# Two transformer blocks on one core: who issues four DRAM copies, who rounds four one-hot tiles, and where the big tiles lie

## The chip, the cores and the metric

One core of one Trainium2 chip runs the whole program. The time is the device time of one execution, in microseconds (us); lower is better. Before the change three executions gave 2247.26 us as their median (2241.52 to 2248.51).

## The reference, cut to what matters

The input is 512 rows of 1024 numbers, all float32. The first block scales and shifts the normalised rows by factors that come from six large "ada" products, projects them with `w_in`, and feeds three mixers: a recurrent one (rwkv), a causal attention with decay (fox) and a sparse attention (nsa). It then projects out and runs a convolutional feed-forward layer. The second block is feed-forward, a token mixer of three more attentions, and feed-forward again.

Four of the attentions add a bias that depends only on the distance between query and key, looked up in a small table of 32 buckets:

```
dist = qpos[:, None] - kpos[None, :]
bias = rel_bias[t5_bucket(dist)]
logits = einsum(q, k) * scale + bias
```

So a bias tile of 128 queries by n keys holds in each row the same line, moved by one element from row to row.

The feed-forward layers are the bulk of the work:

```
u = h @ w_up;  gate, val = split(u);  out = (silu(gate) * val) @ w_down
```

## The kernel before, in words

**Matrix products.** To keep float32 accuracy each operand is split into a high and a low part of a rounded type (float32r), and each product is three matmuls: high by high, low by high, high by low. A weight chunk of 128 x 1024 comes by one DMA into a tile `raw` (three buffers), ScalarE rounds it into `whi` (L273), VectorE or GpSimd makes the rest `wlo` (L274). `Weights.next` does this, and every chunk waits on SyncE's queue for the buffer it will fill. A helper `mm` (L284) issues all matmuls. In `dense` the moving operand of the matmul is an activation: `uh`/`ul` (inputs of a layer), `hh`/`hl` (hidden values of a feed-forward layer, moved in its down product), `oh`/`ol` (attention outputs, in the branch products), `yh`/`yl` (in the output product of the second mixer).

**Ada.** `some_ada` (called between the steps of rwkv) loads 512 KB pieces of the ada weights through the same `raw` buffers, multiplies them on VectorE (`am`, L299), ScalarE and GpSimd (L507, L508, L512), and sums over partitions by a matmul of 128 x 1.

**Bias lines.** `lines` makes the lines: for each 512 columns it loads a one-hot matrix of 33 rows into a tile `lo` (L467), rounds it to float32r (`CAST`, L469), multiplies it by the bias table on TensorE (`pss` in the first block, `lps` in the second), evacuates on ScalarE and stores to a DRAM tensor `d` (L475). There are four such steps in the first block (called from `decays`, beside rwkv) and six in the second (called from `bias_2`, in the first feed-forward layer's up product). `skew` (L477) then copies each line 128 times within DRAM, so that later a DMA can read it back with a step of one element less than a row and get the moved rows. There are four such copies: `k1` (6 lines of 639 numbers, 768 rows written), `k2` (8 lines of 639, 1024 rows), `ka0` (4 lines of 1785, 512 rows of 7140 bytes) and two small ones `ka1` and `ka2` (4 lines of 255 each, 512 rows each). The attentions read them much later: `tb<-k` (L1174) and `bt<-k` (L1614).

**What sets the order.** The engines run their instruction streams in order, and each waits at its next instruction until its inputs are there. A scheduler of the tile framework fixes the order in each stream, so a small change in the code moves neighbours too. All DMAs but four small ones are issued by SyncE, in one stream (`SPq` in the rows), weights and copies alike; GpSimd issues none.

**Where tiles lie.** Pools take room in SBUF one after the other; the `st` pool stands ahead of most others. In the built program of before the tiles `raw`, `whi`, `wlo`, `uh` and `ul` start at multiples of 256 bytes within a partition, `hh` and `hl` 192 bytes past one, `oh`, `ol`, `yh` and `yl` 224 bytes past one.

Of the kernel before, what the change touches and what calls it, by code (L numbers as in the profile page):

```python
# [10 lines left out]
F32 = mybir.dt.float32  # L11
# [7 lines left out]
P = 128  # L19
# [260 lines left out]
def two_blocks(ctx, tc, ins, out):  # L280
    nc = tc.nc
    S, V, G, PE = nc.scalar, nc.vector, nc.gpsimd, nc.tensor
    def mm(o, l, r, start=True, stop=True):
        PE.matmul(o, l, r, start=start, stop=stop)  # L284

    def act(o, i, f, **kw):
        S.activation(o, i, f, **kw)  # L287

    def tt(o, a, b, op):
        V.tensor_tensor(o, a, b, op=op)  # L290
# [7 lines left out]
    def stt(o, a, s, b, op0, op1):  # L298
        V.scalar_tensor_tensor(o, a, s, b, op0=op0, op1=op1)  # L299
# [24 lines left out]
    def vc(name, i=0, n=1):  # L324
        s = VECS[name].start
        return vec[:, s + i:s + i + n]
# [9 lines left out]
    st = ctx.enter_context(tc.tile_pool(name="st", bufs=1))  # L336

    def tmp(name="tmp"):
        return st.tile([P, T], F32, name=name, tag="tmp", bufs=3)
# [7 lines left out]
    def row_sums(ps, accs, start=True, stop=True, s=ALL):  # L347

        n = len(blocks(s))
        for j, acc in enumerate(accs):  # L350
            for i, b in enumerate(blocks(s)):
                mm(ps[:, n * j + i:n * j + i + 1], acc[:, b * P:(b + 1) * P],
                   ones[:, 0:1], start and i == 0, stop and i == n - 1)
        return ps[:, :n * len(accs)]

    def rsq(m, name="rr"):

        n = m.shape[-1]
        v = st.tile([P, NB], F32, name="rv", bufs=2)
        ts(v[:, :n], m, EPS, None, ADD)  # L360
        r = st.tile([P, NB], F32, name=name, bufs=2)
        G.tensor_tensor(r[:, :n], v[:, :n], mhalf[:, :n], op=ALU.pow)
        return r[:, :n]
# [15 lines left out]
    def rms_bcast(psp, tag, r, name="R"):  # L379
        R = st.tile([P, T], F32, name=name)  # L380
        spread(psp, tag, r, R)
        return R
# [22 lines left out]
    def two(k):  # L405
        return slot(UTAG[2 * k], "uh", F32R), slot(UTAG[2 * k + 1], "ul", F32R)
# [8 lines left out]
    def cut_by(t, g, b, hl, s=ALL):  # L415

        h, l = hl[0][:, s], hl[1][:, s]
        if b is None:
            act(h, t, AF.Copy, scale=g)
            stt(l, t, g, h.bitcast(F32), MUL, SUB)  # L420
        else:
            act(h, t, AF.Identity, bias=b)
            stt(l, t, b, h.bitcast(F32), ADD, SUB)
        return hl
# [9 lines left out]
    def dense(ps, hi, lo, k0, us, start=True, stop=True, w=P, s=ALL):  # L434

        n, ps = len(us), ps[:, s]
        for k, (uh, ul) in enumerate(us):
            uh, ul = uh[:, s], ul[:, s]
            a, b = hi[:, k0 + k * w:k0 + k * w + w], lo[:, k0 + k * w:k0 + k * w + w]
            mm(ps, a, uh, start and k == 0, False)  # L440
            mm(ps, a, ul, False, False)
            mm(ps, b, uh, False, stop and k == n - 1)
# [13 lines left out]
    def lines(name, pool, o_tile, pst, rb, n, h, dst):  # L456

        l = pool.tile([33, h], F32, name="rb" + name)
        V.memset(l[32:33, :], 1.0)
        nc.sync.dma_start(l[:32, :], ins[rb])  # L460
        hi, lo = [pool.tile([33, h], F32R, name="rb" + name + c) for c in "hl"]
        act(hi, l, AF.Copy)
        tt(lo, l, hi.bitcast(F32), SUB)
        for j in range(0, n, 512):
            m = min(512, n - j)
            o = o_tile(F32)[:33, :m]
            nc.sync.dma_start(o, ins["lines" + name][:, j:j + m])  # L467
            E = o_tile(F32R)[:33, :m]
            G.tensor_copy(E, o)  # L469
            ps = pst()[:h, :m]  # L470
            mm(ps, hi, E, True, False)
            mm(ps, lo, E, False, True)
            o = o_tile(F32)[:h, :m]
            act(o, ps, AF.Copy)
            nc.sync.dma_start(dst[:, j:j + m], o)  # L475

    def skew(name, src, row0, rows, rstep, off, n):  # L477

        d = dram.tile([rows, P, n], F32, name=name)
        s = src[:]  # L480
        w = s.shape[1]
        nc.sync.dma_start(d, bass.AP(tensor=s.tensor, offset=s.offset + row0 * w + off, ap=[[rstep * w, rows], [0, P], [1, n]]))
        return d

    def skewed(d, h, nh, off, ap):
# [5 lines left out]
    def ada(dst, sec, k, raw, ap, bufs, late):  # L491

        am = [ap.tile([P, 256], F32, name=f"am{q}", bufs=bufs) for q in range(2)]
        n = 4 if late else AN
        for q in range(2):
            aw = raw()
            nc.sync.dma_start(aw.rearrange("p a b -> p (a b)"), ins["ada"][sec, k][:, q * 1024:(q + 1) * 1024])
            for r in range(4):
                s = sil[:, 4 * q + r:4 * q + r + 1]
                if q == 0 and r:  # L500
                    stt(am[0], aw[:, r], s, am[0], MUL, ADD)
                elif q == 0:
                    ts(am[0], aw[:, 0], s, None, MUL)
                elif r == 0:
                    act(am[1], aw[:, 0], AF.Copy, scale=s)
                elif late:
                    G.tensor_scalar(aw[:, r], aw[:, r], s, 1.0, op0=MUL, op1=MUL)  # L507
                    G.tensor_tensor(am[1], am[1], aw[:, r], op=ADD)  # L508
                elif r < n:
                    act(aw[:, r], aw[:, r], AF.Copy, scale=s)  # L510
                    G.tensor_tensor(am[1], am[1], aw[:, r], op=ADD)
        G.tensor_tensor(am[1], am[0], am[1], op=ADD)  # L512
        for s in range(2):
            c = slice(s * P, (s + 1) * P)
            for r in range(n, 4):
                mm(dst[s], aw[:, r, c], sil[:, 4 + r:5 + r], r == n, False)
            mm(dst[s], am[1][:, c], ones[:, 0:1], n == 4, True)
# [20 lines left out]
    with tc.tile_pool(name="lin", bufs=1) as lin, tc.tile_pool(name="p0", bufs=1, space=PSUM) as p0:  # L538
        x0 = part
        for i in range(4):  # L540
            nc.sync.dma_start(x0[:, 2 * i:2 * i + 2], ins["x"][:, 2 * i:2 * i + 2])
        q0 = SqSum()
        for k in range(8):
            q0.add(x0[:, k])
        ps = row_sums(p0.tile([P, T], F32, name="nst", tag="x0"), [q0.acc])
        msx = const.tile([P, NB], F32, name="msx")
        V.tensor_copy(msx, ps[:, :NB])
        R = rms_bcast(p0, "x0", rsq(msx))
        kps = [p0.tile([P, T], F32, name=f"k{m}") for m in range(7)]
        gm = st.tile([P, 8], F32, name="gf")  # L550

        def modulate(k):

            ps = p0.tile([P, T], F32, name="mps", tag="x0")
            ada([ps[:, 0:1], ps[:, 1:2]], 0, k, lambda: lin.tile([P, 4, 256], F32, name="aw", bufs=AWB), lin, 3, False)
            tt(mod[:, k:16:8], ps[:, :2], vc("ada_b", 0, 16)[:, k::8], ADD)
            stt(gm[:, k:k + 1], mod[:, 8 + k:9 + k], 1.0, vc("norm_g", k), ADD, MUL)

        for k in range(8 + LA):
            if k < 8:  # L560
                modulate(k)
            if k < LA:
                continue
            k -= LA
            t = tmp("uf")
            stt(t, x0[:, k], gm[:, k:k + 1], R, MUL, MUL)
            us.append(cut_by(t, None, mod[:, k:k + 1], two(k)))
            hi, lo = W.next("rwkv")
            for m in range(7):
                dense(kps[m], hi, lo, m * P, us[k:k + 1], k == 0, k == 7)  # L570
        for m in range(7):
            act(pr[m], kps[m], AF.Identity, scale=omu[:, m:m + 1])
            stt(pr[m][:, 1:], kps[m][:, :T - 1], vc("mu", m), pr[m][:, 1:], MUL, ADD)
# [4 lines left out]
    def bank(tag, n):  # L578
        return psm.tile([P, T], F32, name="ps" + tag, tag="p" + tag, bufs=n)
# [669 lines left out]
    gf = st.tile([P, 8], F32, name="gf")  # L1249
# [48 lines left out]
    pst, psd, psa, n = bank("t", 2), bank("t", 2), bank("o", 2), 0  # L1298
# [186 lines left out]
    op = blk.enter_context(tc.tile_pool(name="op", bufs=1, reuse_waits="tile"))  # L1485
# [50 lines left out]
        for i in range(2):  # L1536
            evac(i, pn[i])

    gqk = op.tile([P, 3], F32, name="gqk")
    tt(gqk, vc("gain", 0, 6)[:, 0::2], vc("gain", 0, 6)[:, 1::2], MUL)  # L1540
    ts(gqk, gqk, -0.125, None, MUL)

# [213 lines left out]
    with tc.tile_pool(name="cc", bufs=1, reuse_waits="tile") as cc:  # L1756
# [8 lines left out]
        for i in range(1, NB):  # L1765
            n = (i + 1) * P
# [19 lines left out]
        for j in range(2):  # L1786
# [6 lines left out]
            for i in range(NB):  # L1793
                n = (i + 1) * P
# [19 lines left out]
    ap = bc.enter_context(tc.tile_pool(name="ap", bufs=1, reuse_waits="tile"))  # L1814
# [18 lines left out]
    for h in range(4):  # L1833
        po = pO()
        bias = bias_line(k2, h)
        for i in range(NB):
            n = (i + 1) * P
# [14 lines left out]
        o = tmp("ob")  # L1852
# [23 lines left out]
    for j in range(2):  # L1876
# [30 lines left out]
        o = tmp("oa")  # L1907
# [97 lines left out]
```

## Time and profile before

| what | value |
|---|---|
| median of three executions | 2247.26 us (2241.52 to 2248.51) |
| the profiled execution | 2244.32 us, of which the span of its instructions is 2242.5 us |
| TensorE (PE) matmul | 2150.2 us busy, 96% of the span |
| VectorE (DVE) | 1166.0 us, 52% |
| ScalarE (ACT) | 797.9 us, 36% |
| GpSimd (POOL) | 464.6 us, 21% |
| DMA | 238.29 MB moved, mean 106 GB/s |

"Busy" says that an engine has an instruction in work; matmuls overlap each other, so a busy TensorE may still be slower than it could be. What tells that is the distance between the starts of two matmuls. Idle time of an engine that is not the bottleneck costs nothing.

### The profile page before, as it was taken

To read this page: it belongs to the slowest core of one execution; us is meant where nothing else is said; L and a number is where in the kernel's file an instruction comes from. 1 tells how busy PE (TensorE), PEld (TensorE's weight loads), DVE (VectorE), ACT (ScalarE), POOL (GpSimd) and SP (SyncE) were. 2 spreads that over 40 slices of the span, in tenths; PEclk is the share of its full clock that TensorE was granted. 3 is DMA by queue.
4 is the path that set the end of the run, shared out by engine and by line. 5 is a ranking of instruction groups with operands and counts; after the bars stand their busy time and mean duration, and the time that the engine had idled before them with its cause. 6 is when DMAs were issued, how large, how long until landed. Compare 5 with 4: busy or idle time off the path is not lost.

```text
span 2242.5 us, 31600 instructions
## 1 busy us (share of the span) xinstructions
PE 2150.2 (96%) x12444; PEld 1761.4 (79%) x12444; DVE 1166.0 (52%) x2213; ACT 797.9 (36%) x1358; POOL 464.6 (21%) x458
## 2 busy tenths in 40 slices
PE   5988999997979999999999999999999999999999
PEld 4866776666758888878888889998877888888887
DVE  8563444667634465654334438976645455433432
ACT  5432333552523343332123335455444233222321
POOL 5044342334000000131011023242221022100110
PEclk9988998997989999999999999999999999999999
DMA  7246234200433222122222334243161223222222
GB/s 271 86 137 200 96 132 131 58 11 22 163 130 110 94 95 98 70 95 94 94 102 96 115 124 130 95 142 95 66 183 67 95 84 104 100 97 94 94 96 83
DMA packets 83321, 238.29 MB, mean 106 GB/s; under 512 B 10666, under 2 KB 19168, under 8 KB 83044
## 3 DMA queue, kind: packets, MB, share of 16 engines
q1 hardware_dynamic: 82452, 235.69, 31.3%
q8 instruction: 98, 1.61, 0.3%
q10 hardware_dynamic: 720, 0.57, 0.1%
q14 instruction: 51, 0.42, 0.1%
HBM read 216.02 MB, written 15.33 MB: 103 GB/s over the span
## 4 chain that ended last, share of the span: by engine, by line
PE 88%; DMA 6%; DVE 4%; POOL 1%; ACT 1%; issue 1%; SPq 0%; DVEq 0%; POOLq 0%; ACTq 0%
PE mm L284 65%; PE psm L284 5%; PE psr L284 4%; DMA raw<-in_wst_dram 3%; PE pS L284 3%; PE pss L284 2%; PE pO L284 2%; PE pso L284 2%; PE k L284 1%; DMA raw<-in_ada_dram 1%; PE pT L1590 1%; PE pst L1052 1%; PE psa L284 1%; DMA aw<-in_ada_dram 1%; PE pT L1573 1%
## 5 line engine op out<-in xcount | busy, mean ns | idle before, releaser
L273 ACT ACTIVATE whi<-raw 128x1024 fp32r<-128x1024 f32 (+4 forms) x314 | 327.3, 1045 | 838.3 <-PE mm L284 624.3
L274 DVE TENSOR_TENSOR wlo<-raw,whi 128x1024 fp32r<-128x1024 f32 (+4 forms) x302 | 371.5, 1232 | 358.1 <-ACT whi L273 348.3
L284 PE MATMUL mm<-uh,whi 128*128 128x512 f32 (+1 forms) x1296 | 499.5, 391 | 18.8 <-ACT whi L273 15.4
L284 PE MATMUL mm<-ul,whi 128*128 128x512 f32 (+1 forms) x1296 | 504.2, 390 | 5.3 <-DVE ul L299 5.3
L284 PE MATMUL mm<-uh,wlo 128*128 128x512 f32 (+1 forms) x1296 | 504.2, 390 | 1.6 <-DVE wlo L274 1.6
L284 PEld LDWEIGHTS mm<-uh,whi 128*128 128x128 f32 x1296 | 245.1, 191 | 72.2 <-ACT whi L273 17.4
L284 PEld LDWEIGHTS mm<-ul,whi 128*128 128x128 f32 x1296 | 246.4, 190 | 58.5 <-DVE ul L299 8.0
L284 PEld LDWEIGHTS mm<-uh,wlo 128*128 128x128 f32 x1296 | 246.2, 190 | 53.0 <-DVE wlo L274 3.6
L284 PE MATMUL mm<-hl,whi 128*128 128x512 f32 (+1 forms) x550 | 211.6, 385 | 0.0
L284 PE MATMUL mm<-hh,wlo 128*128 128x512 f32 (+1 forms) x550 | 211.6, 385 | 0.0
L284 PE MATMUL mm<-hh,whi 128*128 128x512 f32 (+1 forms) x550 | 210.7, 385 | 0.0
L1441 POOL TENSOR_TENSOR gg<-gg,R 128x512 f32<-128x512 f32 x44 | 76.8, 1748 | 477.6 <-ACT gg L287 477.6
L284 PE MATMUL mm<-whi,uh 128*128 128x256 f32 (+1 forms) x488 | 140.5, 288 | 0.0
L284 PE MATMUL mm<-whi,ul 128*128 128x256 f32 (+1 forms) x488 | 139.7, 286 | 0.0
L284 PE MATMUL mm<-wlo,uh 128*128 128x256 f32 (+1 forms) x488 | 139.2, 285 | 0.0
L284 PEld LDWEIGHTS mm<-hl,whi 128*128 128x128 f32 x550 | 102.9, 187 | 23.6
L284 PEld LDWEIGHTS mm<-hh,wlo 128*128 128x128 f32 x550 | 102.9, 187 | 23.5
L284 PEld LDWEIGHTS mm<-hh,whi 128*128 128x128 f32 x550 | 102.9, 187 | 23.3
L287 ACT ACTIVATE p<-p,smin 128x128 f32<-128x128 f32 (+4 forms) x136 | 81.8, 602 | 74.1 <-DVE smin L1028 38.6
L290 DVE TENSOR_TENSOR gh<-mm,gg 128x512 f32<-128x512 f32 x44 | 30.4, 691 | 130.8 <-PE mm L284 125.3
L284 PEld LDWEIGHTS mm<-whi,ul 128*128 128x128 f32 x488 | 93.1, 191 | 1.7 <-issue 1.5
L284 PEld LDWEIGHTS mm<-whi,uh 128*128 128x128 f32 x488 | 93.0, 191 | 1.3 <-issue 0.4
(506 smaller groups left out, 3407.0 us busy)
## 6 DMA issues: line engine op xcount, KB each, us to landing
raw<-in_wst_dram SPq DMA_DIRECT2D x294, 512.0 KB
raw<-in_ada_dram SPq DMA_DIRECT2D x32, 512.0 KB
aw<-in_ada_dram SPq DMA_DIRECT2D x16, 512.0 KB
raw<-in_wst_dram SPq DMA_DIRECT2D x8, 448.0 KB
ka<-d SPq DMA_DIRECT2D x1, 3570.0 KB
k<-d SPq DMA_DIRECT2D x1, 2556.0 KB
part<-in_x_dram SPq DMA_DIRECT2D x4, 512.0 KB
xa<-in_x_dram SPq DMA_DIRECT2D x8, 256.0 KB
```

Of the source, the lines that this page charges most:

```text
L273: nc.scalar.activation(hi[:, :n], w, AF.Copy)
L274: (e or nc.vector).tensor_tensor(lo[:, :n], w, hi[:, :n].bitcast(F32), op=ALU.subtract)
L284: PE.matmul(o, l, r, start=start, stop=stop)
L287: S.activation(o, i, f, **kw)
L290: V.tensor_tensor(o, a, b, op=op)
L1052: PE.transpose(ps[:, j:j + P], p[:, j:j + P], ident)
L1441: G.tensor_tensor(g, g, R, op=MUL)
L1573: PE.transpose(ps[:, (j * nb + b) * P:(j * nb + b + 1) * P], xn[:, (b * n + j) * P:(b * n + j + 1) * P], ident)
L1590: PE.transpose(ps[:, j:j + P], p[:, o + j:o + j + P], ident)
```

## The change

Three edits. The copies of `skew` are issued by GpSimd instead of SyncE. In `lines` the rounding of the one-hot columns is done by VectorE for the first block (name "1"); the second block stays on GpSimd. Two small tiles are allocated wider and used as before, which moves the tiles allocated behind them.

```diff
@@ -466,7 +466,7 @@
             o = o_tile(F32)[:33, :m]
             nc.sync.dma_start(o, ins["lines" + name][:, j:j + m])
             E = o_tile(F32R)[:33, :m]
-            G.tensor_copy(E, o)
+            (V if name == "1" else G).tensor_copy(E, o)
             ps = pst()[:h, :m]
@@ -479,7 +479,7 @@
         d = dram.tile([rows, P, n], F32, name=name)
         s = src[:]
         w = s.shape[1]
-        nc.sync.dma_start(d, bass.AP(tensor=s.tensor, offset=s.offset + row0 * w + off, ap=[[rstep * w, rows], [0, P], [1, n]]))
+        G.dma_start(d, bass.AP(tensor=s.tensor, offset=s.offset + row0 * w + off, ap=[[rstep * w, rows], [0, P], [1, n]]))
         return d
@@ -547,7 +547,7 @@
-        gm = st.tile([P, 8], F32, name="gf")
+        gm = st.tile([P, 24], F32, name="gf")[:, :8]
@@ -1536,7 +1536,7 @@
-    gqk = op.tile([P, 3], F32, name="gqk")
+    gqk = op.tile([P, 64], F32, name="gqk")[:, :3]
```

Places of tiles in the two built programs, as bytes past a multiple of 256:

| tiles | before | changed |
|---|---|---|
| `raw`, `whi`, `wlo`, `uh`, `ul` | 0 | 0 |
| `hh`, `hl`, `cv`, `part`, `xa`, `xb` (rows of the first and second block's layers) | 192 | 0 |
| `oh`, `ol`, `yh`, `yl`, `bt`, `av`, `xn` (second mixer) | 224 | 0 |
| rwkv's own tiles (`X`, `XT`, `Tm`, `AK`, `WU`) | 0 | 64 |
| tiles of nsa (`qs`, `tb`, `p`, `pt`) | 96 | 160 |

How the instruction streams move. First SyncE's stream in the up product of the first feed-forward layer, at the last of the second block's bias lines (`raw` are weight loads, `d` the lines, `ka` the copies):

```order
 L467 DMA lo<-in_lines_dram 33x374
 L475 DMA d_5927<-lo 20x512
-L269 DMA raw<-in_wst_dram 128x1024
-L482 DMA ka_5997<-d_5927 512x1x1785
-L269 DMA raw<-in_wst_dram 128x1024
+L269 DMA raw<-in_wst_dram 128x1024 x2
 L475 DMA d_5927<-lo 20x374
-L269 DMA raw<-in_wst_dram 128x1024
-L482 DMA ka_5999<-d_5927 512x1x255
-L482 DMA ka_6001<-d_5927 512x1x255
-L269 DMA raw<-in_wst_dram 128x1024 x109
+L269 DMA raw<-in_wst_dram 128x1024 x110
```

The copies have left the stream, and the weight loads behind them follow each other. The same place in GpSimd's stream (`tmp` is the last step ahead of the feed-forward layer, `rr` the first one at its end):

```order
 L1277 TENSOR_TENSOR tmp<-part,R_5289 128x512 x8
-L469 CAST lo<-lo 33x512 x5
+L469 CAST lo<-lo 33x512 x3
+L482 DMA k_5995<-d_5927 1024x1x639
+L469 CAST lo<-lo 33x512 x2
 L469 CAST lo<-lo 33x374
+L482 DMA ka_5997<-d_5927 512x1x1785
+L482 DMA ka_5999<-d_5927 512x1x255
+L482 DMA ka_6001<-d_5927 512x1x255
 L362 TENSOR_TENSOR rr<-rv,mhalf 128x2
```

`k2` now stands ahead of the last three roundings, the other three copies behind all of them. Third, GpSimd's stream beside rwkv (`am` are sums of an ada piece, `raw` the pieces):

```order
 L507 TENSOR_SCALAR raw<-raw,sil 128x256 x6
-L469 CAST lo<-lo 33x512
-L508 TENSOR_TENSOR am_1731<-am_1731,raw 128x256 x3
+L508 TENSOR_TENSOR am_1731<-am_1731,raw 128x256
+L482 DMA k_1237<-d_93 768x1x639
+L508 TENSOR_TENSOR am_1731<-am_1731,raw 128x256 x2
 L512 TENSOR_TENSOR am_1731<-am_1730,am_1731 128x256
-L469 CAST lo<-lo 33x512
```

The roundings are gone from it, and the copy `k1` stands in the middle of one ada sum. TensorE's stream at the last of the first block's bias lines (`psr` are rwkv's small matmuls):

```order
-L284 MATMUL psr_1676<-cm,pr_113 64x64 x16
-L284 MATMUL psr_1694<-cm,pr_114 64x64 x11
+L284 MATMUL psr_1631<-cm,pr_115 64x64 x3
 L284 MATMUL pss<-lo,rb1h 6x96
 L284 MATMUL pss<-lo,rb1l 6x96
-L284 MATMUL psr_1694<-cm,pr_114 64x64 x5
+L284 MATMUL psr_1631<-cm,pr_115 64x64 x13
```

The two matmuls that need the fourth rounded tile stand some 70 small matmuls earlier than before.

## Rows read from the trace of the kernel before

**Rows 1.** The page: span, and busy time and share of each engine.

```profile
span 2242.5 us, 31600 instructions
PE 2150.2 (96%) x12444; PEld 1761.4 (79%) x12444; DVE 1166.0 (52%) x2213; ACT 797.9 (36%) x1358; POOL 464.6 (21%) x458
```

**Rows 2.** The chain that ended last, 610 to 675 us: start, us, what.

```profile
615.51 35.76 DMA raw<-in_wst_dram
...
653.69 14.93 DMA raw<-in_wst_dram
```

**Rows 3.** Timeline of SyncE's queue, 569 to 652 us: start, us, instruction.

```profile
569.97 0.73 SPq L482 DMA_DIRECT2D k<-d  x1
...
611.35 0.69 SPq L482 DMA_DIRECT2D ka<-d  x1
...
651.47 2.11 SPq L482 DMA_DIRECT2D ka<-d  x2
```

**Rows 4.** Stretches of the feed-forward layers: busy us and count by engine.

```profile
core 0: us, PE busy (x) PEld busy (x) DVE busy (x) ACT busy (x) POOL busy (x), PEclk, DMA share, GB/s
570.00:600.00 30.00, 30.00 (x131) 23.59 (x131) 16.96 (x22) 12.12 (x18) 1.40 (x1) 1.00 0.53 179
615.70:688.70 73.00, 57.94 (x233) 46.06 (x233) 29.27 (x37) 20.57 (x28) 0.00 (x0) 0.88 0.37 127
635.00:645.00 10.00, 6.22 (x28) 4.82 (x26) 0.00 (x0) 0.00 (x0) 0.00 (x0) 0.98 0.25 104
750.30:869.90 119.60, 119.60 (x529) 99.07 (x528) 70.41 (x84) 51.09 (x65) 0.00 (x0) 1.00 0.28 97
916.20:927.40 11.20, 11.20 (x100) 11.20 (x99) 4.41 (x8) 2.53 (x4) 0.00 (x0) 1.00 0.15 48
1812.50:1829.20 16.70, 16.70 (x73) 13.47 (x72) 12.59 (x14) 4.99 (x6) 8.44 (x5) 1.00 0.22 75
1829.30:1874.50 45.20, 45.15 (x193) 35.82 (x192) 25.80 (x28) 17.06 (x23) 8.52 (x4) 1.00 0.27 95
2177.10:2238.50 61.40, 61.40 (x265) 49.15 (x263) 16.98 (x18) 10.06 (x10) 0.00 (x0) 1.00 0.23 82
```

**Rows 5.** Timeline of TensorE, single matmuls of 256 and of 512 columns.

```profile
944.51 0.28 PE L284 MATMUL mm<-uh,whi 128*128 128x256 f32 x1
...
946.91 0.28 PE L284 MATMUL mm<-uh,wlo 128*128 128x256 f32 x1
...
1995.76 0.39 PE L284 MATMUL mm<-hh,whi 128*128 128x512 f32 x1
...
1999.96 0.39 PE L284 MATMUL mm<-hh,whi 128*128 128x512 f32 x1
```

**Rows 6.** Timelines beside rwkv, 169 to 190 us: SyncE's queue, GpSimd, TensorE.

```profile
169.41 0.85 SPq L482 DMA_DIRECT2D k<-d  x1
177.30 1.24 SPq L497 DMA_DIRECT2D raw<-in_ada_dram  x2
...
188.06 0.93 POOL L507 TENSOR_SCALAR raw<-raw,sil 128x256 f32<-128x256 f32 x2 [9.85 <-DMA raw<-in_ada_dram]
188.93 0.26 POOL L469 CAST lo<-lo 33x96 fp32r<-33x96 f32 x1
...
189.24 0.24 PE L284 MATMUL pss<-lo,rb1h 33*6 33x96 f32 x1 [9.46 <-POOL lo L469]
```

**Rows 7.** Stretches beside rwkv, columns as in rows 4.

```profile
180.00:190.00 10.00, 0.76 (x11) 0.60 (x12) 0.71 (x2) 0.24 (x1) 1.59 (x4) 0.69 0.57 211
190.00:198.00 8.00, 8.00 (x73) 6.46 (x70) 2.82 (x6) 3.24 (x5) 6.32 (x8) 0.54 0.52 136
```

**Rows 8.** GpSimd's timeline at 594 us, VectorE's at 118 us.

```profile
594.53 1.40 POOL L469 CAST lo<-lo 33x512 fp32r<-33x512 f32 x1 [24.76 <-DMA lo<-in_lines_dram]
...
118.04 0.43 DVE L684 COPY nr<-hr 128x512 f32<-128x512 f32 x1 [1.75 <-POOL hr L682]
```

**Rows 9.** Line L1614, the reads of `k2`: count, issue ns, first and last start.

```profile
L1614 SPq DMA_DIRECT2D bt<-k x8: 319/332/424, 1309.3 to 1549.9; - x8
```

## What the change should do to the time

> **What bounds the kernel now.** I read the page first: TensorE has a matmul in work for 96% of the span, no other engine for more than 52% [rows 1]. So time is won only where TensorE stands still, where its clock is granted at half, or where its matmuls follow each other more slowly than they could. Next I read the chain that ended last. In the feed-forward layers it is TensorE all the way, but for two pieces of 35.76 and 14.93 us that are weight loads, issued at 615.51 and 653.69 [rows 2]. SyncE's queue shows what stands just ahead of each: the copy `ka0` at 611.35 and the copies `ka1` and `ka2` from 651.47 [rows 3]. Between 635 and 645 the DMA engines are busy a quarter of the time although weights are waited for [rows 4]: the copy of 4 lines runs on 4 of 16 engines, and a weight load that needs all 16 ends only when those 4 have finished it. Third, I compared stretches in which TensorE runs without a pause, for the distance between matmuls, and the stretch beside rwkv where it stood still longest.
>
> **Term 1, the two stalls at 615 to 689.** The stretch 615.7 to 688.7 holds 232 matmuls (the count less the one that began before it) in 73.0 us. The stretch 750.3 to 869.9 has the same matmuls at 119.6/528 = 0.2265 us each [rows 4]. 232 of these take 52.5 us, so 20.5 us are lost, in standing still and at a clock of 0.88 on average. The change takes the copies off SyncE's queue and leaves TensorE's order there as it was. If a copy issued by GpSimd stands in another queue, the weights share the 4 engines with it rather than wait for its end. An estimate: the copy occupies its engines from 615.5 to about 651.3, in 512 rows, so a row takes about 35.8 x 4 / 512 = 0.28 us; a weight load puts 8 rows of 4096 bytes on an engine. Even if one row of the copy ran between any two rows of the weights, 8 rows of each would take some 3.5 us (a weight row counted at 0.16 us, from its share of the bytes), and a load is used up in 24 matmuls, 5.4 us. With three buffers that keeps up. I take the whole 20.5 us; ends 0 (still in line) and 20.5. `k2`, issued at 569.97, costs nothing now, since TensorE is busy throughout 570 to 600 [rows 3, 4].
>
> **Term 2, the place of the tiles.** In down products the moving operand `hh` lies 192 bytes past a multiple of 256, in up products `uh` lies on one. The up stretch gives 0.2265 us a matmul; the down stretch 2177.1 to 2238.5 gives 61.4/264 = 0.2326 from the window, and single starts give (1999.96 - 1995.76)/18 = 0.2333 [rows 4, 5]. Weights, stationary tiles and widths are alike. That the place is what matters and not the kind of product is shown by `oh` in the branch stretch, 16.7/72 = 0.2319, and `yh` in the output stretch, 45.2/192 = 0.2354 [rows 4]: both lie 224 bytes past a multiple, and the output product is written like an up product. The difference is 6.7 ns (0.2333 less 0.2266, as the tighter reading). Of 512 columns there are 6 down products of 8 x 11 x 3 less 66, that is 1518, with `hh`/`hl`, and 192 each with `oh` and `yh`: 1902 x 6.7 ns = 12.7 us. Against this, the 132 matmuls of 256 columns in the last two tiles of the first layer now run at 11.2/99 = 0.1131 us, while those of `uh`, on a multiple, run at (946.91 - 944.51)/20 = 0.1200: a loss of 0.9 us. Sum 11.8 us gained, as TensorE has no other pause in these stretches. The weights must then come every 5.4 us instead of 5.6, which the up stretches already do at a DMA share of 0.28 [rows 4]. Ends: 0, if the place is a coincidence, and 13. ScalarE's and VectorE's work on the moved tiles I cost at nothing, hidden behind TensorE; that of rwkv, whose tiles go from 0 to 64 bytes, stays in the bounds of term 3, as no row tells how it behaves.
>
> **Term 3, the stretch beside rwkv.** `k1` is issued at 169.41; an ada load issued behind it at 177.30 lets GpSimd go on only at 188.06, and GpSimd's fourth rounding, in line behind that ada work, comes at 188.93; TensorE's `pss` waited 9.46 us for it [rows 6]. From 180 to 190 TensorE is busy 0.76 us, and the next 8 us run at a clock of 0.54 [rows 7], so about 9.2 + 8.0 x 0.46 = 12.9 us are lost. The change removes both links: `k1` no longer stands ahead of the ada load, and the rounding, now VectorE's, no longer stands behind ada work. The four roundings cost VectorE about 4 x 0.43 = 1.7 us, by its copy of 128 x 512 [rows 8], beside rwkv's own steps. But ada work itself is still due: behind `k1` in GpSimd's stream stand the rest of an ada sum, whose small matmul TensorE takes in order, and all later sums. What is late next is that sum, and GpSimd now waits for the lines to land and issues 768 rows itself. SyncE's issue took 0.85 us; at most, if GpSimd is held until the copy is done, 18.7 us (169.41 to 188.06) [rows 6]. No row shows a copy issued by GpSimd; I take 5 us, nearer to an issue than to a transfer, with part of it on the path. Of 12.9 us I count 7 as gained. Ends: 13 gained, and 18.7 - 12.9 = 5.8 lost.
>
> In the feed-forward layer the roundings stay on GpSimd behind `k2`: the fourth begins at 594.53, 24.6 us after `k2` is issued now [rows 3, 8], so it is covered up to that hold. Behind `ka0` to `ka2` GpSimd has nothing until that layer ends, and `k2` is first read at 1309.3 [rows 9], hundreds of us later: longer copies cost nothing there.
>
> **Sum.** The profiled execution took 2244.3 us, 1.8 of them outside its span. 2244.3 - 20.5 - 11.8 - 7 = 2205.0. It lies 2.9 us below the median of the three runs and inside their range; I go one us up for that: 2206.
>
> **Rivals.**
>
> *The weights still wait (0.14).* Against the estimate of term 1: the engines are the same 16, and if each serves a long run of copy rows before it turns to the weights, the stall only changes its place. Then term 1 shrinks to between 0 and 10: 2216 to 2226. [...] The quarter share at 635 [rows 4] agrees with the common engines; no run here shows yet how two queues take turns.
>
> *The place does nothing (0.10).* Products with `hh` differ from those with `uh` also in who wrote the operand and when. Then term 2 is 0: 2217. Against it speak `oh` and `yh`.
>
> *GpSimd is held at `k1` (0.09).* As bounded above, up to the whole transfer: term 3 turns to +5.8 and the time to 2218.
>
> *Slower (0.05).* GpSimd needs so long for each row of a copy that ada sums and roundings come late. With X the time a row, `k1` holds it 768 X and `k2` 1024 X, of which 24.6 us are covered. Gains of 20.5 + 11.8 + 12.9 = 45.2 are eaten when 1792 X = 69.8 us, at X = 39 ns; the bound of 18.7 us gives 24. At 50 ns the kernel takes 2244.3 - 45.2 + 38.4 + 26.6 = 2264. [...]
>
> *No change (0.04).* The copies wait in line as before and the place does nothing: 2237 to 2250, partly within 0.3% (6.7 us), which is what a measurement of this kernel can tell from no change.
>
> **Chances and range.** The forecast, all three terms at about their size, has 0.58 and lies between 2197 (13 in terms 2 and 3) and 2212. The first three rivals are faster too: 0.58 + 0.14 + 0.10 + 0.09 = 0.91, less 0.02 for pairs of them. So faster 0.89, same 0.06, slower 0.05. The range goes from 2195 (all upper ends, at the lowest of the runs) to 2229 (the weights wait and `k1` gives nothing: 2244.3 - 11.8 - 0, less 3); about 0.15 is left out.
>
> **What would show it.** Term 1: TensorE's 232 matmuls after the last `lps` take about 53 us at full clock, and no weight load of over 10 us is left in the chain there. Term 2: matmuls with `hh`, `oh`, `yh` start 0.2265 us apart, those of 256 columns 0.120. Term 3: no wait of TensorE for a rounding, and the first NSA read of `k1` some 7 us earlier; if instead GpSimd shows a long wait or a long issue at L482, the third or fourth rival holds. The forecast is wrong if weight loads still land late while a copy runs, or if the down stretches keep 0.2333.

## The result and the profile after

| kernel | median | executions | ratio to before, 95% interval |
|---|---|---|---|
| before, timed beside it | 2244.55 us | 4 (2241.52 to 2248.51) | |
| changed | 2213.38 us | 4 (2211.90 to 2214.77) | 0.9858 [0.9844, 0.9872] |

The changed kernel is 31.2 us faster. The prediction said 2206 (2195 to 2229). The profiled execution took 2211.9 us where the sum of the prediction gave 2205.0; nearly the whole difference of 6.9 us is the third term, as the rows show.

The page of the changed kernel: span, busy time of TensorE, the DMA queues. Against [rows 1] TensorE is busy 13 us less and its share of the span has risen by one percentage point; the copies now stand in a queue of their own, `q0`.

```profile
span 2210.1 us, 31599 instructions
PE 2137.1 (97%) x12444; PEld 1764.5 (80%) x12444; DVE 1167.0 (53%) x2217; ACT 799.1 (36%) x1358; POOL 465.2 (21%) x459
...
q1 hardware_dynamic: 79098, 226.41, 30.5%
q0 software_dynamic: 5008, 9.31, 1.2%
```

**Term 1.** The chain that ended last, 600 to 680 us, in the changed kernel: start, us, what. The two pieces of weight loads of [rows 2] are gone; behind the last `lps` TensorE runs without a break.

```profile
614.95 0.45 PE lps L284 x2
615.40 64.60 PE mm L284 x284
```

**Terms 1 and 2.** Windows of the changed kernel, columns as in [rows 4], at the places that answer to its second, fifth, sixth, seventh and last row.

```profile
615.40:667.80 52.40, 52.40 (x232) 43.40 (x232) 31.70 (x39) 22.34 (x29) 2.16 (x2) 1.00 0.58 186
...
892.20:904.10 11.90, 11.90 (x100) 11.87 (x99) 4.63 (x8) 2.52 (x4) 0.00 (x0) 1.00 0.13 45
...
1785.00:1801.30 16.30, 16.30 (x74) 13.50 (x73) 12.58 (x14) 4.99 (x6) 8.30 (x4) 1.00 0.21 69
...
1801.40:1845.40 44.00, 43.89 (x193) 35.76 (x192) 26.59 (x28) 17.05 (x23) 8.42 (x4) 1.00 0.31 100
...
2146.20:2205.90 59.70, 59.70 (x265) 49.36 (x263) 16.98 (x18) 10.10 (x10) 0.00 (x0) 1.00 0.23 84
```

The matmuls after the last `lps` take 52.4 us at full clock instead of 73.0. The down stretch takes 59.7/264 = 0.2261 us a matmul by its window, which has an uncertainty of one matmul at each end. Single starts are tighter; these are from TensorE's timeline of the changed kernel, two of 256 columns and two of 512.

```profile
892.58 0.28 PE L284 MATMUL mm<-hh,whi 128*128 128x256 f32 x1
...
894.74 0.28 PE L284 MATMUL mm<-hh,whi 128*128 128x256 f32 x1
...
2160.49 0.39 PE L284 MATMUL mm<-hh,whi 128*128 128x512 f32 x1
...
2164.57 0.39 PE L284 MATMUL mm<-hh,whi 128*128 128x512 f32 x1
```

18 matmuls lie between the two of a pair: 2.16/18 = 0.1200 us at 256 columns, 4.08/18 = 0.2267 us at 512, where [rows 5] gave 0.2333. Both are the numbers that the prediction named. The windows with `oh` and `yh` have gone from 16.7 to 16.3 and from 45.2 to 44.0 us.

**Who issues the copies.** GpSimd's timeline of the changed kernel, the rows of L482, and the last line of the view of L482.

```profile
165.19 1.33 POOL L482 DMA_DIRECT2D k<-d  x1
...
569.70 1.18 POOL L482 DMA_DIRECT2D k<-d  x1 [0.42 <-DMA d<-lo]
...
610.48 1.10 POOL L482 DMA_DIRECT2D ka<-d  x1 [3.14 <-DMA d<-lo]
624.12 2.16 POOL L482 DMA_DIRECT2D ka<-d  x2 [12.54 <-DMA d<-lo]
...
DMA to landing us min/median/max: 20.6/38.7/51.5
```

An issue holds GpSimd 1.1 to 1.3 us, whether the copy has 512 or 1024 rows, and it goes on while the copy needs 20 to 50 us to land. So the third and the fourth rival fell: 1.18 us for 1024 rows is 1.2 ns a row, where 39 would have made the kernel slower.

**Term 3.** Beside rwkv the old wait is gone and another has come. SyncE's timeline of the changed kernel, 173 to 189 us, then TensorE's.

```profile
173.92 0.29 SPq L475 DMA_DIRECT2D d<-lo  x1
...
181.69 4.52 SPq L935 DMA_DIRECT2D cb<-d  x8
...
188.23 1.08 SPq L980 DMA_DIRECT2D w<-in_ck_dram  x2
```

```profile
183.61 0.91 PE L284 MATMUL psr<-X,part 64*64 64x64 f32 x22
191.65 0.66 PE L284 MATMUL psa<-kr,w 128*128 128x62 f32 x2 [7.13 <-DMA w<-in_ck_dram]
```

`cb` reads the bias lines back, so it waits until the last piece `d`, issued at 173.92, has landed (2.9 us of SyncE's waits at L935); its eight loads go out from 181.69 on, and `w`, the weights of the compression in nsa (`psa` is its matmul), stands behind them. TensorE waits 7.13 us for it at 191.65.

How much that took back is seen in one wide window, 140 to 230 us, of before and of the changed kernel, and in two pieces of the changed one.

```profile
140.00:230.00 90.00, 74.24 (x1055) 61.80 (x1054) 46.36 (x94) 24.84 (x44) 47.25 (x67) 0.89 0.57 186
```

```profile
180.00:191.70 11.70, 4.57 (x72) 3.74 (x70) 2.24 (x6) 1.89 (x4) 6.98 (x12) 0.83 0.64 183
191.70:207.00 15.30, 15.30 (x118) 13.56 (x120) 3.87 (x9) 2.82 (x3) 6.05 (x11) 0.50 0.68 227
140.00:230.00 90.00, 78.29 (x1056) 65.55 (x1056) 45.62 (x97) 24.29 (x42) 44.70 (x64) 0.85 0.58 186
```

By 230 us TensorE has begun 1055 matmuls in the one and 1056 in the other. It stood still 4 us less in the changed kernel (78.29 busy against 74.24), and gave that back in clock, 0.85 against 0.89 on average: from 191.7 to 207 it was granted 0.50 for 15.3 us behind the new wait, where [rows 7] show 8 us at 0.54 behind the old one.

Further on nothing was gained either. Of each of the next pairs the first line is from the kernel before, the second from the changed one: the reads of `k1` in nsa, then the first matmuls of the second block's bias lines, at the start of the feed-forward layer (count, ns, first and last start).

```profile
L1174 SPq DMA_DIRECT2D tb<-k x6: 326/411/589, 381.2 to 425.7; - x6
L1174 SPq DMA_DIRECT2D tb<-k x6: 327/404/587, 382.2 to 426.9; - x6
...
L284 PE MATMUL lps<-lo,rb2h x6: 340/400/402, 557.9 to 615.3; 33*20 33x512 f32 x5, 33*20 33x374 f32 x1
L284 PE MATMUL lps<-lo,rb2h x6: 347/410/410, 557.4 to 614.9; 33*20 33x512 f32 x5, 33*20 33x374 f32 x1
```

The first read of `k1` comes 1.0 us later, where the prediction expected it some 7 us earlier, and `lps` begins 0.5 us earlier.

### The profile page after: what moved, and what is told of

It reads as the page before. It is cut to its first block, busy times and chain, and to the rows that moved or that the text cites. A ratio compares the mean times of both kernels' runs of the same rounds, so it can differ in the third digit from the quotient of the medians.

```text
span 2210.1 us, 31599 instructions
## 1 busy us (share of the span) xinstructions
PE 2137.1 (97%) x12444; PEld 1764.5 (80%) x12444; DVE 1167.0 (53%) x2217; ACT 799.1 (36%) x1358; POOL 465.2 (21%) x459
## 4 chain that ended last, share of the span: by engine, by line
PE 91%; DVE 4%; DMA 3%; ACT 1%; issue 1%; POOL 1%; SPq 0%; DVEq 0%; ACTq 0%; POOLq 0%
PE mm L284 67%; PE psm L284 6%; PE psr L284 4%; PE pS L284 3%; PE pss L284 2%; PE pso L284 2%; PE pO L284 2%; PE k L284 1%; PE psa L284 1%; PE pT L1590 1%; PE pst L1052 1%; DMA aw<-in_ada_dram 1%; DMA raw<-in_wst_dram 1%; PE pT L1573 1%; DVE ul L299 1%
## 6 DMA issues: line engine op xcount, KB each, us to landing
k<-d POOLq DMA_DIRECT2D x1, 2556.0 KB, 20.6
```

## The experiments

Each was timed beside the kernel before on its chip; the medians of before there were 2246.05 (first four), 2247.53 (next four) and 2246.93 us (last four). The changed kernel's time is the one of the table above, beside 2244.55; so differences of 1 to 2 us between an experiment and the changed kernel say nothing.

**1. The second block's copies alone.**

```diff
 def skew(...):                       # kernel before
-    nc.sync.dma_start(d, ...)
+    (nc.sync if name == "k1" else G).dma_start(d, ...)
```

> The kernel before, with only the second block's four copies (k2, ka0 to ka2) issued by GpSimd; k1, the roundings and all tile places as before. TensorE's, VectorE's and ScalarE's streams are those of before. Theory (each copy stalls the weights that stand behind it in SyncE's queue): the 231 matmuls after the last lps take 52 to 53 us instead of 72.7, the time falls by 20 to 21 us to 2223.5 to 2225, and nothing else moves. Rival (the stall went only because the tiles also moved, or part of it comes back later in the layer): a gain of 10 to 17 us, 2228 to 2235.

Measured: 2227.57 us (2223.52 to 2227.64), ratio 0.9909 [0.9895, 0.9923], a gain of 18.5 us. The window behind the last `lps`:

```profile
618.80:671.00 52.20, 52.20 (x231) 43.22 (x231) 31.70 (x39) 22.36 (x29) 2.16 (x2) 1.00 0.62 188
```

The stretch is what the theory asked for, 52.2 us; the time missed its range (2223.5 to 2225) by 2.6 us. In the profiled execution what is missing lies ahead of the copies: `lps` begins at 560.9 instead of 557.9, although up to there the streams are those of before. So two executions of the same order differ by some 3 us up to that point, which the later experiments must be read against.

**2. The places alone.**

```diff
-        gm = st.tile([P, 8], F32, name="gf")
+        gm = st.tile([P, 24], F32, name="gf")[:, :8]
-    gqk = op.tile([P, 3], F32, name="gqk")
+    gqk = op.tile([P, 64], F32, name="gqk")[:, :3]
```

> The kernel before, with only the two small tiles allocated wider, so that hh, hl, oh, ol, yh, yl start at multiples of 256 bytes and rwkv's tiles 64 past one. All engine streams are those of before. Theory (the place of the moving operand sets the distance between matmuls, and rwkv's tiles don't care): 512-column matmuls with hh and oh 226.7 ns apart, the 256-column ones with hh 120, a gain of 11.5 to 12.5 us, 2232 to 2233. Rival A (the change of place costs the rwkv stretch what term 3 was to bring): the stretch up to 318 us becomes 3 to 7 us longer and the gain is only 5 to 9 us, 2235.5 to 2239.5. Rival B (the pitch in the changed kernel comes from the order and not from the place): 2244, no gain.

Measured: 2234.51 us (2231.18 to 2235.47), 0.9944 [0.9930, 0.9958], a gain of 11.5 us. The last down stretch, with the streams of before:

```profile
2167.90:2227.50 59.60, 59.60 (x265) 49.36 (x264) 16.98 (x18) 10.10 (x10) 0.00 (x0) 1.00 0.24 84
```

61.4 us have become 59.6 with no instruction moved: the place is the cause, and rivals A and B fall (`lps` begins at 556.5, so rwkv does not pay for its tiles' new place).

**3. `cb` after rwkv.** If the wait behind `cb` had eaten term 3, taking it away should give the 7 us.

```diff
 ...
         lines("1", keep, ...)
-        load_cb()
         k1.append(skew("k1", d1, 0, 6, 1, 0, LN))
 ...
     att = blk.enter_context(tc.tile_pool(name="att", ...))
+    cb = att.tile([P, 6, 55], F32, name="cb")
+    ...
+    load_cb()
```

> The changed kernel, with the eight loads of cb (L935), which in it hold SyncE's queue from 173.9 to 187 us because they wait for the last piece of d1 to land, done after rwkv into a tile of the attention's pool; tile places of all large tiles as in the changed kernel. Theory (term 3 was eaten by this wait: TensorE's psa at 191.65 waits 7.1 us for w, which stands behind cb in SyncE's queue): that wait shrinks to under 2 us, the end of the rwkv stretch comes 4 to 8 us earlier, the time is 2205.5 to 2209.5. Rival (the end of the stretch is set by something else, the ada sums or rwkv's own chain, and any wait removed in it only moves on): the wait goes, the end of the stretch stays within 1.5 us, the time is 2212 to 2215.

Measured: 2205.51 us (2204.69 to 2206.60), 0.9817 [0.9803, 0.9831]: 7.9 us less than the changed kernel, as the theory's number said, and yet its reason falls. TensorE's waits of this kernel, 170 to 235 us (who, for what: us in total, times, longest):

```profile
PE psa L284 <- POOL kr L975: 8.5, 2, 7.2
PE psa L284 <- DMA w<-in_cv_dram: 1.3, 1, 1.3
```

The wait for `w` is gone and one for `kr` of 7.2 us has taken its place, and TensorE's first matmul of nsa's attention (`pss<-kct`) begins at 375.8, as in the changed kernel (375.7). So the rival is right about the stretch and wrong about the time (2212 to 2215). The gain came later: `lps` begins at 550.9 instead of 557.4. The order of loads and of the weights' low parts in nsa's attention and in the passage to the feed-forward layer had moved too.

**4. `k1` back on SyncE, roundings on VectorE.**

```diff
 def skew(...):                       # changed kernel
-    G.dma_start(d, ...)
+    (nc.sync if name == "k1" else G).dma_start(d, ...)
```

> The changed kernel, with k1 alone issued by SyncE again; the first block's roundings stay on VectorE, the second block's copies on GpSimd, the places as changed. Theory (what stands in front of TensorE's next input in SyncE's queue decides in this stretch, so k1 there delays ada and weight loads behind it as before): 3 to 9 us slower than the changed kernel, 2216 to 2222, with a new wait of TensorE of 5 us or more before 195 us. Rival (the stretch ends when rwkv's own chain and the ada sums end, whatever waits lie inside): within 1.5 us of the changed kernel, 2212 to 2215.

Measured: 2214.84 us (2211.42 to 2217.95), 0.9858 [0.9841, 0.9875], 1.5 us from the changed kernel, whose ratio is the same. TensorE's longest wait, 140 to 230 us:

```profile
PE pss L284 <- DVE lo L469: 8.4, 2, 8.2
```

A wait of 8.2 us, and the 3 to 9 us of the theory did not come: again a wait of some 8 us near this place, under another name. The time is the rival's.

**5. `k1` at 250 us.** Next theory: the stretch is short of bytes, and the 2 MB of `k1` are in the way.

```diff
-        k1.append(skew("k1", d1, 0, 6, 1, 0, LN))
+    d1b = dram.tile([6, LN], F32, name="d1b")
+    def late_k1(spare):
+        ...                              # lines -> SBUF -> d1b (two small DMAs)
+        k1.append(skew("k1", d1b, 0, 6, 1, 0, LN))
 ...
         turn[0] += 1
+        if turn[0] == 16:
+            late_k1(spare)
```

> The changed kernel, with k1 (1.9 MB of rows) taken out of the stretch beside rwkv: its source is a copy of the lines that is made later, so that GpSimd issues it at about 250 us, where the DMA engines are busy 0.2 to 0.3 of the time. In the third experiment the wait behind cb went, TensorE then waited 7.2 us for kr, and the stretch ended where it had, so the wait behind cb was not what set its end. Theory now (up to about 215 us the stretch is fed at what the DMAs bring, 15 to 16 MB in 140 to 220 us in every variant, so 2 MB less bring the rest 10 us sooner): TensorE's standing still and half clock before 230 us shrink, the end of the stretch comes 5 to 10 us earlier, the time is 2203 to 2208.5. Rival (the end is set by the chain of ada sums and rwkv's steps themselves, each waiting for the one before): the end within 2 us, the time 2211.5 to 2215.

Measured: 2214.17 us (2212.83 to 2218.98), 0.9852 [0.9837, 0.9868]. The wide window, then TensorE's waits for `w` in it (us in total, times, longest), of which one is its longest there:

```profile
140.00:230.00 90.00, 80.92 (x1059) 67.50 (x1058) 46.89 (x101) 24.78 (x44) 45.44 (x64) 0.84 0.54 170
```

```profile
PE psa L284 <- DMA w<-in_ck_dram: 2.6, 2, 2.3
```

The bytes are gone from it (170 GB/s instead of 186), TensorE stands still less, its clock is lower still, and it has begun 1059 matmuls by 230 us, three more than with `k1` there. The theory falls, and the time is the rival's. That the stretch ends within 2 us of where it did is not shown: in the profiled execution, 4.8 us above the median, nsa's attention begins at 384.4 instead of 375.7. Here no wait of 7 us is left in the stretch, and the kernel is still no faster.

**6. Both.** The edits of 3 and 5 together.

> Both: k1 at about 250 us and cb after rwkv. In the third experiment the gain of 7.9 us arose behind rwkv (2.1 us at the start of the sparse attention near 400 us, 4 us in the passage to the feed-forward layer near 510 us), where the order of loads and of the low parts of the weights differs. Theory (those gains belong to the order behind rwkv and add to what the fifth experiment brings): 6 to 8 us below the fifth experiment. Rival (they were owed to when rwkv ended and don't add): within 2 us of the better of the third (2205.5) and the fifth.

Measured: 2212.38 us (2210.36 to 2217.70), 0.9846 [0.9828, 0.9865]. Neither the theory nor its rival: 1.8 us below the fifth and 6.9 above the third. Moving `cb` does not bring the 7.9 us of the third by itself; that they belong to the order of the streams there is likely, and not shown.

**7. All copies on ScalarE.**

```diff
-    G.dma_start(d, ...)
+    S.dma_start(d, ...)
```

> The changed kernel, with all copies issued by ScalarE instead of GpSimd; roundings on VectorE for the first block, places as changed. Theory (what counts is that the copies leave SyncE's queue, whoever issues them): the 231 matmuls after the last lps take 52 to 54 us, the time is within 3 us of the changed kernel, 2211 to 2216. Rival (DMAs of SyncE and of ScalarE are served in one line by each DMA engine, and only GpSimd's are not): weights land late behind ka0 again, those matmuls take 65 to 73 us, the time is 2224 to 2235.

Measured: 2230.95 us (2230.63 to 2236.05), 0.9931 [0.9917, 0.9946], slower than the changed kernel by 17.6 us and in the rival's range. The 231 matmuls behind the last `lps` take 69.5 us (617.7 to 687.2), in its range too. The rival's reason is not in the rows, though. ScalarE's timeline, then its waits from 610 to 690 us:

```profile
612.54 0.61 ACTq L482 DMA_DIRECT2D ka<-d  x1
...
626.84 0.61 ACTq L482 DMA_DIRECT2D ka<-d  x1
...
627.77 27.93 ACTq L482 DMA_DIRECT2D ka<-d  x1
655.75 0.63 ACT L287 ACTIVATE hh<-cv 128x512 fp32r<-128x512 f32 x1 [27.42 <-issue]
```

```profile
ACT hh L287 <- issue: 27.4, 1, 27.4
```

ScalarE never waits for `raw` here: the weights pass. It stands 27.9 us at its own issue of `ka2`, 15 us behind `ka0` in the same queue, and TensorE lacks the `whi` that ScalarE makes, 14.3 us in one wait (`ka1`, just ahead of it, went out in 0.61 us). SyncE had been held in the same way before the change. This is its first weight load behind `ka0`, from SyncE's timeline of the kernel before:

```profile
615.51 13.57 SPq L269 DMA_DIRECT2D raw<-in_wst_dram  x1
```

So part of the stall of [rows 2] was SyncE standing at an issue. Whether ScalarE's loss was such a hold alone is for the ninth experiment.

**8. Places at 64.** On the changed kernel.

```diff
-        gm = st.tile([P, 24], F32, name="gf")[:, :8]
+        gm = st.tile([P, 40], F32, name="gf")[:, :8]
```

> The changed kernel, with the first small tile another 64 bytes wider, so that hh, hl, oh, ol, yh and yl start 64 bytes past a multiple of 256 and rwkv's tiles 128 past one; the streams are those of the changed kernel. Theory (any place off a multiple of 256 costs a matmul of 512 columns some 6 ns): hh 512 columns 231 to 234 ns apart, oh and yh likewise, time 2221 to 2226. Rival (only 192 and 224 cost, or a multiple of 64 bytes is enough): 226.7 ns, time 2211 to 2215.

Measured once: 2217.74 us. Two starts, 18 matmuls apart, in the same down stretch: 4.12/18 = 0.2289 us, between 0.2267 and 0.2333. Two starts of 256 columns, at 895.51 and 897.63, 18 matmuls apart, give 0.1178. Neither the theory (231 to 234 ns, 2221 to 2226 us) nor the rival (226.7 ns, 2211 to 2215 us) holds. The 0.2289 is a mean: by the starts in nanoseconds the three matmuls of a product follow each other at 0.232, 0.226 and 0.229 us in turn.

```profile
2160.36 0.39 PE L284 MATMUL mm<-hh,whi 128*128 128x512 f32 x1
...
2164.48 0.39 PE L284 MATMUL mm<-hh,whi 128*128 128x512 f32 x1
```

**9. `ka0` alone on ScalarE.**

```diff
-    G.dma_start(d, ...)
+    (S if n > 1000 else G).dma_start(d, ...)
```

> The changed kernel, with ka0 alone issued by ScalarE and the other four copies by GpSimd; streams otherwise those of the changed kernel. In the seventh experiment ScalarE never waited for a weight load from 610 to 690 us; it stood 27.4 us at the issue of ka1 and ka2, which came 15 us after ka0 in the same queue. Theory (a queue of another engine lets the weights by, and the loss there was the issue of a further copy, held until ka0 had gone through): with nothing behind ka0 in ScalarE's queue the 231 matmuls after the last lps take 52 to 54 us and the time is 2211 to 2216. Rival (SyncE's weights and ScalarE's copy stand in one line at each DMA engine): 62 to 73 us, 2222 to 2234, with waits of ScalarE for raw as before the change.

Measured: 2211.98 us (2210.11 to 2214.80), 0.9848 [0.9833, 0.9862], the time of the changed kernel. ScalarE's issue, and the window behind the last `lps`:

```profile
613.05 1.19 ACTq L482 DMA_DIRECT2D ka<-d  x1
```

```profile
618.20:670.50 52.30, 52.30 (x232) 43.32 (x232) 29.11 (x36) 19.98 (x26) 2.18 (x2) 1.00 0.48 160
```

The theory holds: a large copy on ScalarE's queue lets SyncE's weights by, and what it cost in experiment 7 was the hold at a further issue behind it. That `ka0` left SyncE's queue is worth some 20 us in this stretch, 52.3 us instead of 73.0, where its issue alone took 0.69 us there [rows 3].

**10. The axes of the copies exchanged, still on SyncE.**

```diff
-        nc.sync.dma_start(d, bass.AP(..., ap=[[rstep * w, rows], [0, P], [1, n]]))
+        o = d[:]
+        nc.sync.dma_start(bass.AP(tensor=o.tensor, offset=o.offset, ap=[[n, P], [P * n, rows], [1, n]]),
+                          bass.AP(..., ap=[[0, P], [rstep * w, rows], [1, n]]))
```

> The kernel before, all copies still issued by SyncE at the same places, with the axes of each copy exchanged: 128 repeats outermost and the lines inside, so that the same rows can be shared out to 16 engines instead of 4 (ka0 to ka2), 6 (k1) or 8 (k2). Theory (the stall was the weights' wait for the few engines that carried a copy): ka0 needs about 35.8 x 4 / 16 = 9 us, which the three weight buffers (16 us) nearly cover, so the 231 matmuls take 53 to 58 us instead of 72.7 and that stretch gives back 15 to 20 us of the 20.4; with up to 3 us either way beside rwkv the time is 2224 to 2233. Rival (a copy within DRAM is limited by its rows or by DRAM, not by the number of engines, or the axes don't set who carries it): no gain, 2240 to 2250.

Measured: 2220.63 us (2218.33 to 2222.09), 0.9887 [0.9871, 0.9904], a gain of 26.3 us over before, more than expected. The window behind the last `lps`, and two lines of the DMA view from 605 to 616 us; below them the same two lines of the kernel before from 616 to 650, while `ka0` runs. Both windows hold weight loads beside the copy.

```profile
610.50:662.80 52.30, 52.30 (x231) 43.32 (x232) 31.67 (x39) 22.24 (x29) 0.00 (x0) 1.00 0.65 176
```

```profile
DMA packets 479, 2.92 MB, mean 265 GB/s; under 512 B 16, under 2 KB 16, under 8 KB 479
...
q1 hardware_dynamic: 479, 2.92, 95.7%
```

```profile
DMA packets 744, 4.36 MB, mean 128 GB/s; under 512 B 34, under 2 KB 46, under 8 KB 742
...
q1 hardware_dynamic: 742, 4.33, 34.1%
```

All engines carry the copy now, 95.7% busy, where a quarter of them was busy with the 4 lines outermost [rows 4], and the whole stall of [rows 2] goes without a second queue. The rest, some 5 us, is gained ahead of it: `lps` begins at 552.5 instead of 557.9, more than the 3 us by which executions differ.

**11. The change without its two edits in the first block.** Experiments 1 and 2 together, on the kernel before.

> The kernel before with the second block's copies on GpSimd and the places changed, that is the change without its two edits in the first block (k1 on SyncE, roundings on GpSimd). Theory (beside rwkv one wait took the place of another, and these edits are worth nothing): within 3 us of the changed kernel, 2210.5 to 2216.5. Rival (they are worth the 7 us that term 3 counted, and something else lost them): 2218 to 2223.

Measured: 2213.11 us (2210.39 to 2215.13), 0.9851 [0.9836, 0.9866]: the changed kernel's time to 0.3 us, with the intervals 3 us either way. The 7 us of the rival are not there; the two edits are worth nothing that these runs can tell.

**12. Places at 128.** On the changed kernel.

```diff
-        gm = st.tile([P, 24], F32, name="gf")[:, :8]
+        gm = st.tile([P, 56], F32, name="gf")[:, :8]
```

> The changed kernel with hh, hl, oh, ol, yh and yl 128 bytes past a multiple of 256 (rwkv's tiles 192). So far matmuls with hh of 512 columns are 226.7 ns apart at 0, 229.0 at 64 and 233.3 at 192 bytes, those of 256 columns 119.9, 117.8 and 113.1. Theory (the distance grows in proportion to the place, 2.2 to 2.3 ns for 64 bytes, and falls likewise for 256 columns): 231.0 to 231.6 and 115.0 to 116.0 ns, time 2219 to 2224. Rival (steps: one level up to half of 256, one beyond): 229.0 or 233.3 ns.

Measured once: 2224.27 us. Two starts 15 matmuls apart: 3.50/15 = 0.2333 us, the mean that 192 has. At 512 columns the theory of proportion falls, and the mean is the rival's second value. It isn't one level, though: by the starts in nanoseconds single distances alternate between 0.229 and 0.238 us here, where at 192 nearly all are 0.233 or 0.234. At 256 columns two starts, 895.91 and 897.69, 15 matmuls apart, give 0.1187, above the theory's 0.115 to 0.116 and above the 0.1178 at 64. What rule the distance follows stays open.

```profile
2160.07 0.40 PE L284 MATMUL mm<-hh,wlo 128*128 128x512 f32 x1
...
2163.57 0.39 PE L284 MATMUL mm<-hh,wlo 128*128 128x512 f32 x1
```

## Why the prediction was right, and where it was not

**Term 1** (20.5 us): 73.0 - 52.4 = 20.6 us. Right in size, and the first rival fell. The reason holds in its main point, four engines held (a DMA share of 0.25 in [rows 4]) by a copy that stands in line with the weights: experiments 9 and 10 remove either half, the line or the four engines, and each removes the whole stall (52.3 us in both). What the reason lacks is that SyncE itself stood at the issue behind `ka0`, 13.57 us of the first piece.

**Term 2** (11.8 us): from the end of that stretch to the end of the span the kernel before takes 2242.5 - 688.7 = 1553.8 us, the changed one 2210.1 - 667.8 = 1542.3, so 11.5 us less; alone in experiment 2 it is 11.5 us too. The place is the cause, and the loss at 256 columns came as named (0.1200). The second rival fell.

**Term 3** is the step that failed: "Of 12.9 us I count 7 as gained." It gave nothing: `lps` begins 0.5 us earlier, and experiment 11 has the same time without its two edits. The links that it named were removed as it said. What was wrong is its answer to what is late next. It named the ada sum and GpSimd's issue, and GpSimd's issue costs 1.3 us; the next wait was in SyncE's stream, where `w` stands behind the eight loads of `cb` and these behind the landing of `d`. The prediction listed what stood behind the wait on GpSimd, and didn't follow SyncE's stream past the rows that left it. It also priced a wait by its own length and the clock behind the old one: the new wait is 2.3 us shorter (7.13 against 9.46), but TensorE ran at half clock for 15.3 us behind it, not 8.

Whether removing the new wait would have brought the 7 us is answered as far as these runs go: no. Four orders of this stretch (the changed kernel and experiments 3, 4 and 11) each show one wait of TensorE of 7 to 10 us between 170 and 192 us, for `w`, `kr`, the rounded tile on VectorE and that on GpSimd (10.1). Experiments 5 and 6 have no single wait above 2.3 and 3.9 us from 140 to 230 us. In them a late step of rwkv (the first `psr<-NF,MT`) starts at 303.0 and 300.7 instead of 304.1, little beyond what executions of one order differ by, and their times lie within 1 us of the changed kernel. Nsa's attention begins between 374.4 and 379.2 us in the profiled executions of all kernels but two: experiment 10 (370.9) and experiment 5 (384.4, in an execution 4.8 us above its median). What sets that end is not settled. Against the bytes of `k1` speaks experiment 5; the chain of ada sums and rwkv's own steps remains and wasn't taken apart. Nor is it known why the order of experiment 3 is 6.6 us faster between 376 us and the start of `lps`.

The third experiment's kernel, at 2205.5 us, is faster than the changed one. Exchanged axes together with the new places weren't run; the gains of experiments 10 and 2 add up to 37.8 us, so an estimate for them is 2209 us, without the second queue.

## What to carry to other kernels

When an inner wait is removed, follow every queue, the DMA queue first, to the next thing that the same engine will want, and count the low clock behind a wait with it (15.3 us at 0.50 here); where orders with and without a wait take the same time, the wait is a symptom. Give a large copy in line with weight loads an axis that all 16 engines can share, or a queue in which nothing else is urgent: either took 73.0 us to 52.3 here (experiments 10 and 9). Compare the distance between matmuls stretch by stretch: equal shapes at different distances (0.2333 and 0.2267 us here) can point to the place of the operands, and moving the tiles alone tests it.

## What the runs showed of the hardware that was not expected

- The mean distance of 512-column matmuls with `hh` as moving operand depends on where it starts past a multiple of 256 bytes: 0.2267 us at 0, 0.2289 at 64, 0.2333 at 128 and at 192 (one execution each at 64 and 128). At 256 columns an offset makes them closer: 0.1200 at 0, 0.1178 at 64, 0.1187 at 128, 0.113 at 192.
- A DMA issued behind a large copy in the same queue held ScalarE 27.9 us (experiment 7) and SyncE 13.57 us (kernel before); GpSimd issued `ka1` and `ka2` in 2.16 us behind the same copy.
- While the 3.6 MB copy within DRAM ran, weight loads included, the DMA engines were 34% busy at 128 GB/s, or 96% at 265 GB/s, by the order of the copies' axes alone (experiment 10).
